# Hybrid encoder trunk on one core: other pairs of the up-projection in seven products, sums and subtractions in turn, gate convolution and silu one step later

## The chip, the cores and the metric

The kernel runs on one core of a Trainium2 chip. The metric is the device time of one execution in microseconds (us). A core has TensorE (PE in the profile; its weight loads are a row of their own, PEld), VectorE (DVE), ScalarE (ACT), GpSimd (POOL) and SyncE (SP), which issues most of the DMAs. Each engine works through a queue of its own in order and waits for the others by semaphores. On-chip memory has 128 partitions; matmuls add up in PSUM tiles (`acc`, `ps`).

## The reference

Two layers over 256 positions of width 2048. Each layer is a token mixer (attention of one kind or the other) and a gated MLP with a convolution over positions. The change lies in the MLP (`conv_ffn`), the first in layer 0 (FFN0), the second in layer 1 (FFN1).

```python
def conv_ffn(h, w_up, conv_w, conv_b, w_down):
    """Gated MLP with centred depthwise conv over positions; h: [B,S,D]."""
    u = h @ w_up
    ...
    u = lax.conv_general_dilated(u, conv_w[:, None, :].astype(u.dtype), window_strides=(1,),
                                 padding=((pad, pad),), dimension_numbers=('NWC', 'WIO', 'NWC'),
                                 feature_group_count=c) + conv_b
    gate, val = jnp.split(u, 2, axis=-1)
    return (jax.nn.silu(gate) * val) @ w_down

def reference(x, a_w_qkv, a_w_o, a_q_gain, a_k_gain, b_w_qkv, b_w_o, rel_bias,
              mix_norm, ffn_norm, w_up, conv_w, conv_b, w_down, final_norm):
    h = x
    for i in range(DEPTH):
        hn = rms_norm(h, mix_norm[i])
        j = i // N_MIXERS
        if i % N_MIXERS == 0:
            h = h + mixer_a(hn, a_w_qkv[j], a_w_o[j], a_q_gain[j], a_k_gain[j])
        else:
            h = h + mixer_b(hn, b_w_qkv[j], b_w_o[j], rel_bias)
        h = h + conv_ffn(rms_norm(h, ffn_norm[i]), w_up[i], conv_w[i], conv_b[i], w_down[i])
    return rms_norm(h, final_norm)
```

All inputs and the output are float32.

## The kernel before

**Split matmuls.** Every float32 operand is split into a rounded part and a remainder, and a product is made of three matmuls: rounded by rounded, rounded by remainder, remainder by rounded (lines 130 to 132, and 184 to 186 in a unit). Weights arrive by DMA as `raw`, tiles of 128 x 1024. For each tile ACT copies the rounded part (`wh`, lines 142 and 177) and VectorE subtracts it from `raw` to get the remainder (`wl`, lines 143 and 178; a "subtraction", S below). There are four buffers of `wh` and of `wl` and four of `raw`, with a few more in the MLP. These two instructions have a raised priority (`AHEAD`), so that the scheduler puts them ahead of work that the program states earlier; each engine's order is settled when the program is built.

**Feeds.** `feed` takes one group of 512 weight rows (a k-group, `kg`) by 512 columns: two tiles of `raw`, 24 matmuls. A plain pair of the up-projection is a block of 512 gate columns (four feeds) and the block of 512 value columns that belongs to it (four feeds), 192 matmuls. There are 11 pairs, numbered 0 to 10, worked in two halves (`HALVES`): pairs 0 to 5, then the part of the down-projection that reads them, then pairs 6 to 10 and theirs.

**Units.** For the pairs that `UP` names, `up_pair` replaces the two feeds of k-group 0, 48 matmuls, by one `fast_unit` of 42: seven products of 2 x 2 blocks in the manner of Strassen and Winograd, out of seven weights. Four of the seven are sums of raw tiles, made in place by VectorE (line 176; a "sum", A below). The order within such a pair (`UP_ORDER`) is gate k-groups 1, 2, 3, the unit, value k-groups 1, 2, 3. The seven products are put together by VectorE in PSUM and in `fold` (lines 690 to 698). On the side of the activations the unit needs recombined inputs of k-group 0 (`picks`), which `sums` prepares once per half with small VectorE rows (lines 649 and 657).

**The work behind the matmuls.** When a gate block is summed up, `gate_gen` evacuates it (ACT, line 486, into `stg`), turns it (`turned`: two transposes of VectorE, line 374, and 16 copies of POOL, line 559, into `u`), and goes on with the value of the pair before: its convolution (ACT line 538, VectorE line 546) and its product with the gate (line 574). When a value block is summed up, `value_gen` evacuates and turns it, waits a number of steps, convolves the gate of its own pair, applies silu (line 583), and splits the product of the pair before for the down-projection (`act_split`, lines 601 and 602). In the last pair of each half, half of the copies that turn the value go to ACT (line 561). For two k-groups of the down-projection in each half (`fast`: those of pairs 1 and 2, 7 and 8) `act_split` calls `combined` instead, which forms differences (line 612) and splits them (lines 317 and 318, tiles `s`, `sx` and `c`), since the down-projection works these two k-groups with `fast_unit` too.

**What sets the order.** These generators advance at each `yield`. A feed calls `step` two times for the oldest of the waiting generators, a unit three times; when one is done, the next one's turn comes. How many yields stand in a generator thus says how many half feeds later a piece is stated in the program. The scheduler then orders each engine's queue by what is stated, by priority and by data.

Of the kernel before, what the change touches and what calls it, by code (L numbers as in the profile page):

```python
# [22 lines left out]
SCALE = 128.0 ** -0.5  # L23
NRAW, NHL = 4, 4
AHEAD = 60
UP = 1, 4, 6, 7, 10
UP_ORDER = (1, 0), (2, 0), (3, 0), (0, None), (1, 1), (2, 1), (3, 1)
NWARM = 11
QC = [(q, c) for q in range(4) for c in range(4)]
# [4 lines left out]
def tile_encoder(ctx: ExitStack, tc: tile.TileContext, x, xT, w_a, w_ao, q_gain, k_gain, w_b, w_bo,  # L34
                 rel_bias, gains, w_up, conv, w_down, final_norm, rope, ident_c, onehot, out):
    nc = tc.nc
# [64 lines left out]
    def raw_tile():  # L101
# [4 lines left out]
            return pool.tile([P, 2, 512], F32, tag=tags[0], name=nm("raw"), bufs=2 if len(tags) == 1 else 1)  # L106
        return spool.tile([P, 2, 512], F32, tag="raw", name=nm("raw"), bufs=NRAW)

    def of_m(x, m):
        return x[m] if isinstance(x, tuple) else x[:, m * P:(m + 1) * P]  # L110

    def feed(accs, lhs, kg, wap, first, last, by_m=False, pieces=1, mid=None, begun=()):
        raws, w = [], 2048 // pieces
        for i in range(max(pieces, 2)):
            if pieces < 4 or i % 2 == 0:
                raws.append(raw_tile())
            w = min(w, 1024)
            r = raws[-1].rearrange("p a c -> p (a c)")
            k = i % 2 if pieces == 4 else 0
            nc.sync.dma_start(r[:, k * w:(k + 1) * w], wap[:, i * w:(i + 1) * w])  # L120
            if mid is not None:
                mid(i)

        def mms(order):
            for m, kt in order:
                (wh, wl), j = hls[kt // 2], kt % 2
                xh, xl = lhs[4 * kg + kt][:2]
                st, sp = first and kt == 0 and m not in begun, last and kt == 3
                xh, xl = of_m(xh, m), of_m(xl, m)
                nc.tensor.matmul(accs[m], xh, wh[:, j, :], start=st, stop=False)  # L130
                nc.tensor.matmul(accs[m], xh, wl[:, j, :], start=False, stop=False)  # L131
                nc.tensor.matmul(accs[m], xl, wh[:, j, :], start=False, stop=sp)  # L132

        hls = []
        for s in range(2):
            wh = spool.tile([P, 2, 512], F32R, tag="wh", name=nm("wh"), bufs=NHL)
            wl = spool.tile([P, 2, 512], F32R, tag="wl", name=nm("wl"), bufs=NHL)
            r = raws[s]
            with tc.high_priority(offset=AHEAD):
                for i in range(max(pieces // 2, 1)):  # L140
                    c = slice(i, i + 1) if pieces == 4 else slice(0, 2)
                    nc.scalar.activation(wh[:, c], r[:, c], AF.Copy)  # L142
                    nc.vector.tensor_tensor(wl[:, c], r[:, c], wh[:, c].bitcast(F32), ALU.subtract)  # L143
            hls.append((wh, wl))
            if not by_m:
                for kt in (2 * s, 2 * s + 1):
                    mms([(m, kt) for m in range(2)])
                    step(kt % 2 == 0)
        if by_m:
            mms([(m, kt) for m in range(2) for kt in range(4)])  # L150
# [11 lines left out]
    def fast_unit(acc, pick, wap0, wap1, begun, end, spot):  # L162
        def load(wap, i):
            r = raw_tile()
            nc.sync.dma_start(r.rearrange("p a c -> p (a c)"), wap[:, i * 1024:(i + 1) * 1024])
            return r

        b11, b21, b22, b12 = load(wap0, 0), load(wap0, 1), load(wap1, 1), load(wap1, 0)
        t1, t2, t4 = (b11, b22, b21) if spot is None else (spot(i) for i in range(3))
        sums = {3: (t1, b11, b12), 5: (b12, b12, b22), 7: (t2, t1, b22), 6: (t4, t2, b21)}  # L170
        for i, (q, r) in enumerate(((1, b11), (2, b21), (3, b22), (5, t1), (7, b12), (6, t2), (4, t4))):
            wh = spool.tile([P, 2, 512], F32R, tag="wh", name=nm("wh"), bufs=NHL)
            wl = spool.tile([P, 2, 512], F32R, tag="wl", name=nm("wl"), bufs=NHL)
            with tc.high_priority(offset=AHEAD):
                if q in sums:
                    nc.vector.tensor_tensor(*sums[q], ALU.add)  # L176
                nc.scalar.activation(wh, r, AF.Copy)  # L177
                nc.vector.tensor_tensor(wl, r, wh.bitcast(F32), ALU.subtract)  # L178
            xh, xl = pick[q]
            for j in range(2):  # L180
                st = q not in begun and j == 0
                sp = q in end and j == 1
                a, b = (x[j] if isinstance(x, tuple) else x[:, j] for x in (xh, xl))
                nc.tensor.matmul(acc[q], a, wh[:, j], start=st, stop=False)  # L184
                nc.tensor.matmul(acc[q], a, wl[:, j], start=False, stop=False)  # L185
                nc.tensor.matmul(acc[q], b, wh[:, j], start=False, stop=sp)  # L186
            begun.add(q)
            step(i % 2 == 0)
# [300 lines left out]
    def ffn(l, hT, ss_in, cw, g_next, last, side=None):  # L489
        with tc.tile_pool(name=nm("fpool"), bufs=1) as fp:  # L490
# [44 lines left out]
            def conv(blk):  # L535
                n, u, c = blk
                for j in range(4):
                    tc.keep_in_program_order(nc.scalar.activation(  # L538
                        halves(c[:, j]), u[:, j, :, :P], AF.Identity, bias=tap(n, j, 3), scale=tap(n, j, 1)))
                    if j == 1:  # L540
                        yield
                flat = u.rearrange("p j m t -> p j (m t)")
                for j in range(4):
                    cj = halves(c[:, j])
                    for i, o in ((0, 0), (2, 1)):
                        nc.vector.scalar_tensor_tensor(cj, halves(flat[:, j, o:o + NT])[:, ::-1], tap(n, j, i), cj,  # L546
                                                       ALU.mult, ALU.add)
                    if j == 1:
                        yield
# [13 lines left out]
            def gate_gen(accs, blk, value):  # L563
                s = evac_scaled(fp, accs, rstd, 1)
                yield
                turned(s, blk[1])
                if value is not None:
                    yield
                    yield from product(value)

            def product(value):
# [4 lines left out]
            def value_gen(accs, blk, gate, last):  # L576
                s = evac_scaled(fp, accs, rstd, 1)
                yield
                turned(s, blk[1], blk[0] - NPAIR in (HALVES[0][1] - 1, NPAIR - 1))
                for _ in range(3 if gate[0] in UP else 1 if last else 4):  # L580
                    yield
                yield from conv(gate)
                nc.scalar.activation(gate[2], gate[2], AF.Silu)
                if last is not None:
                    yield
                    yield from act_split(last)
# [59 lines left out]
            def sums(kg, at, r, st):  # L646
                hts = [hT[4 * kg + j][:2] for j in range(4)]
                for j, (hi, lo) in enumerate(hts):
                    nc.vector.tensor_tensor(r[:, j], hi.bitcast(F32), lo.bitcast(F32), ALU.add)
                    if j == 1:  # L650
                        yield
                v = r.rearrange("p (b j) (m t) -> p b j m t", b=2, m=2)
# [854 lines left out]
```

## Time and profile before

| what | value |
|---|---|
| median of 3 runs | 2250.79 us (2250.02 to 2251.2) |
| profiled execution | 2250.06 us, span 2248.3 us, mean granted clock 0.998 |
| VectorE: subtractions of feeds, x708 | 887.1 us busy, mean 1264 ns |
| VectorE: subtractions of units out of raw tiles, x126 | 154.8 us busy, mean 1256 ns |
| POOL: copies that turn gate and value, x672 | 519.4 us busy, mean 773 ns |
| DMA from HBM | 432.34 MB read, 195 GB/s over the span |

Times are microseconds unless marked ns. A row of the timeline gives start, duration, engine, line and operation, output and inputs, shapes, how many rows of one kind it merges (x4), and in brackets the idle time before it with what ended it. A row of the waits gives the waiting engine and line, what it waited for, the idle time in total, how often, and the longest. A row of the windows gives the stretch, its length, the busy time of PE, PEld, DVE, ACT and POOL with counts, the granted clock of TensorE, the share of the DMA engines and GB/s. A row of the groups gives busy time, mean ns of one, and idle time before them. Matmul starts are what tells TensorE's pace, since matmuls overlap.

### The profile page before, as it was taken

Reading aid. Unit: us, or ns where it says so; the run is one execution under the profiler, and the core shown is the slowest. Engines: PE = TensorE matmul, PEld = TensorE weight load, DVE = VectorE, ACT = ScalarE, POOL = GpSimd, SP = SyncE. Lnnn points to the kernel's source line nnn. Section 1 sums busy time; section 2 is a strip of 40 time slices with the busy share of each in tenths; the row PEclk is TensorE's granted clock in tenths of the full one; section 3 lists DMA queues with packets and bytes.
Section 4 is the critical chain, followed back from the end, with each engine's and each line's share of the span. In section 5 each row is a group of like instructions: output and inputs, shape, how many; then the busy total and the mean of one; then the engine's idle time right before and its main releaser. Section 6 shows DMA issues by size and latency. Waiting matters only on the chain.

```text
span 2248.3 us, 28923 instructions
## 1 busy us (share of the span) xinstructions
PE 2217.8 (99%) x9945; PEld 1833.1 (82%) x9945; DVE 1905.6 (85%) x2415; ACT 1351.5 (60%) x1902; POOL 761.5 (34%) x1017
## 2 busy tenths in 40 slices
PE   9999999999999999999999999999999999999998
PEld 7888878888887887888888888888788878878877
DVE  6877779898899989868886878687999998898987
ACT  7676665666455656665454455566666755565664
POOL 2343236652005662040053006003665500347511
PEclk9999999999999999999999999999999999999999
DMA  8565655556556546565556555556455555556654
GB/s 303 193 217 175 218 184 201 184 199 195 205 190 208 192 163 212 198 187 197 189 186 196 179 187 184 195 185 212 171 205 196 193 198 197 200 189 202 208 187 142
DMA packets 126181, 439.60 MB, mean 196 GB/s; under 512 B 14408, under 2 KB 18248, under 8 KB 126032
## 3 DMA queue, kind: packets, MB, share of 16 engines
q1 hardware_dynamic: 123056, 429.05, 56.5%
q0 software_dynamic: 2688, 8.39, 1.5%
q8 instruction: 78, 1.28, 0.2%
q14 instruction: 71, 0.58, 0.1%
q10 hardware_dynamic: 288, 0.30, 0.0%
HBM read 432.34 MB, written 5.34 MB: 195 GB/s over the span
## 4 chain that ended last, share of the span: by engine, by line
PE 46%; DVE 5%; issue 2%; DMA 1%; POOL 1%; ACT 1%; DVEq 0%; POOLq 0%; ACTq 0%
PE acc L132 13%; PE acc L130 13%; PE acc L131 13%; DVE wl L143 2%; PE ps L185 1%; PE ps L186 1%; PE ps L184 1%; DVE wl L178 1%; DMA raw<-in_w_b_dram 1%; PE acc L185 1%; PE acc L186 1%; DMA raw<-in_w_up_dram 1%; PE acc L184 1%; DVE raw L176 1%; ACT wh L142 1%
## 5 line engine op out<-in xcount | busy, mean ns | idle before, releaser
L143 DVE TENSOR_TENSOR wl<-raw,wh 128x1024 fp32r<-128x1024 f32 (+1 forms) x708 | 887.1, 1264 | 192.6 <-ACT wh L142 187.7
L142 ACT ACTIVATE wh<-raw 128x1024 fp32r<-128x1024 f32 (+1 forms) x708 | 738.9, 1048 | 505.7 <-PE acc L132 393.9
L131 PE MATMUL acc<-wl,xh 128*128 128x512 f32 x2016 | 785.6, 390 | 1.7 <-DVE wl L143 1.7
L130 PE MATMUL acc<-wh,xh 128*128 128x512 f32 x2016 | 786.3, 390 | 0.7 <-ACT wh L142 0.7
L132 PE MATMUL acc<-wh,xh 128*128 128x512 f32 x2016 | 784.5, 389 | 0.0
L559 POOL COPY u<-quad 32x256 f32<-32x256 f32 x672 | 519.4, 773 | 451.8 <-DVE quad L374 414.9
L131 PEld LDWEIGHTS acc<-wl,xh 128*128 128x128 f32 x2016 | 378.6, 188 | 80.6 <-DVE wl L143 4.1
L130 PEld LDWEIGHTS acc<-wh,xh 128*128 128x128 f32 x2016 | 378.8, 188 | 78.5 <-ACT wh L142 1.1
L132 PEld LDWEIGHTS acc<-wh,xh 128*128 128x128 f32 x2016 | 378.5, 188 | 78.8
L130 PE MATMUL acc<-wh,a 128*128 128x512 f32 x720 | 281.7, 391 | 1.6 <-ACT a L601 1.6
L132 PE MATMUL acc<-wh,a 128*128 128x512 f32 x720 | 281.0, 390 | 0.6 <-DVE a L602 0.6
L131 PE MATMUL acc<-wl,a 128*128 128x512 f32 x720 | 281.0, 390 | 0.0
L177 ACT ACTIVATE wh<-raw 128x1024 fp32r<-128x1024 f32 x126 | 133.2, 1060 | 115.0 <-PE acc L132 95.8
L130 PEld LDWEIGHTS acc<-wh,a 128*128 128x128 f32 x720 | 135.8, 189 | 30.0 <-ACT a L601 2.5
L132 PEld LDWEIGHTS acc<-wh,a 128*128 128x128 f32 x720 | 135.5, 188 | 29.7 <-DVE a L602 1.4
L131 PEld LDWEIGHTS acc<-wl,a 128*128 128x128 f32 x720 | 135.6, 188 | 28.2 <-DVE wl L143 0.4
L178 DVE TENSOR_TENSOR wl<-raw,wh 128x1024 fp32r<-128x1024 f32 x126 | 154.8, 1256 | 1.5 <-ACT wh L177 0.9
L378 POOL COPY wide<-quad 32x256 f32<-32x256 f32 x133 | 90.1, 678 | 168.2 <-DVE quad L374 159.8
L395 POOL COPY wide<-quad 32x256 f32<-32x256 f32 x88 | 53.1, 603 | 240.2 <-DVE quad L374 173.0
L546 DVE SCALAR_TENSOR_TENSOR cg<-u,cw,cg 128x256 f32<-128x256 f32 x176 | 88.3, 542 | 11.3 <-ACT cg L538 11.0
L486 ACT ACTIVATE stg<-acc,rstd 128x512 f32<-128x512 f32 x122 | 80.5, 680 | 24.7 <-DVE acc L693 12.1
L546 DVE SCALAR_TENSOR_TENSOR cv<-u,cw,cv 128x256 f32<-128x256 f32 x176 | 85.4, 532 | 0.0
(309 smaller groups left out, 2275.5 us busy)
## 6 DMA issues: line engine op xcount, KB each, us to landing
raw<-in_w_up_dram SPq DMA_DIRECT2D x352, 512.0 KB, 4.6
raw<-in_w_down_dram SPq DMA_DIRECT2D x176, 512.0 KB, 4.5
raw<-in_w_b_dram SPq DMA_DIRECT2D x144, 512.0 KB, 4.4
raw<-in_w_bo_dram SPq DMA_DIRECT2D x48, 512.0 KB, 4.4
raw<-in_w_a_dram SPq DMA_DIRECT2D x40, 512.0 KB, 4.7
raw<-in_w_ao_dram SPq DMA_DIRECT2D x32, 512.0 KB, 4.6
raw<-in_w_a_dram SPq DMA_DIRECT2D x16, 256.0 KB, 5.8
there<-quad POOLq DMA_DIRECT2D x6, 512.0 KB, 4.0
```

Source lines behind the costliest of these rows:

```text
L130: nc.tensor.matmul(accs[m], xh, wh[:, j, :], start=st, stop=False)
L131: nc.tensor.matmul(accs[m], xh, wl[:, j, :], start=False, stop=False)
L132: nc.tensor.matmul(accs[m], xl, wh[:, j, :], start=False, stop=sp)
L142: nc.scalar.activation(wh[:, c], r[:, c], AF.Copy)
L143: nc.vector.tensor_tensor(wl[:, c], r[:, c], wh[:, c].bitcast(F32), ALU.subtract)
L177: nc.scalar.activation(wh, r, AF.Copy)
L178: nc.vector.tensor_tensor(wl, r, wh.bitcast(F32), ALU.subtract)
L378: nc.gpsimd.tensor_copy(o[32 * c:32 * c + 32, :, 32 * q:32 * q + 32], quad[32 * q:32 * q + 32, c])
L395: nc.gpsimd.tensor_copy(dst, src)
L486: nc.scalar.activation(o[:, m, :], accs[m], AF.Copy, scale=rstd[:, m:m + 1])
L546: nc.vector.scalar_tensor_tensor(cj, halves(flat[:, j, o:o + NT])[:, ::-1], tap(n, j, i), cj, ALU.mult, ALU.add)
L559: nc.gpsimd.tensor_copy(o, src)
```

## The change

`UP` names pairs 2, 4, 6, 7 and 8 instead of 1, 4, 6, 7 and 10: five units per layer as before, three of them in a row in the second half. In the units of the up-projection each sum is issued after the subtraction before it (`issue_after`), and `sums` ties its four additions behind the newest subtraction of a feed. In `gate_gen` the value of pair 0 is convolved one step later. In `value_gen` the number of steps ahead of the gate's convolution becomes 4 instead of 3 for a unit's pair, 2 instead of 1 for a plain pair with another before it in its half, and 5 instead of 4 for a plain pair that opens a half; one step more stands ahead of silu.

```diff
-UP = 1, 4, 6, 7, 10
+UP = 2, 4, 6, 7, 8
...
+    newest = [None]
...
-                    nc.vector.tensor_tensor(wl[:, c], r[:, c], wh[:, c].bitcast(F32), ALU.subtract)
+                    newest[0] = nc.vector.tensor_tensor(wl[:, c], r[:, c], wh[:, c].bitcast(F32), ALU.subtract)
...
                 if q in sums:
-                    nc.vector.tensor_tensor(*sums[q], ALU.add)
+                    with tc.issue_after(done.ins) if spot is None else ExitStack():
+                        nc.vector.tensor_tensor(*sums[q], ALU.add)
                 nc.scalar.activation(wh, r, AF.Copy)
-                nc.vector.tensor_tensor(wl, r, wh.bitcast(F32), ALU.subtract)
+                done = nc.vector.tensor_tensor(wl, r, wh.bitcast(F32), ALU.subtract)
...
                 if value is not None:
-                    yield
+                    for _ in range(2 if blk[0] == 1 else 1):
+                        yield
                     yield from product(value)
...
-                for _ in range(3 if gate[0] in UP else 1 if last else 4):
+                for _ in range(4 if gate[0] in UP else 2 if last else 5):
                     yield
                 yield from conv(gate)
+                yield
                 nc.scalar.activation(gate[2], gate[2], AF.Silu)
...
                 for j, (hi, lo) in enumerate(hts):
-                    nc.vector.tensor_tensor(r[:, j], hi.bitcast(F32), lo.bitcast(F32), ALU.add)
+                    with tc.issue_after(newest[0].ins):
+                        nc.vector.tensor_tensor(r[:, j], hi.bitcast(F32), lo.bitcast(F32), ALU.add)
```

The counts of instructions are the same on every engine, and so is the order of SP's DMA issues. In the changed file line numbers are two to six higher: L145 and L181 are the subtractions, L179 the sum, L541 and L549 the convolution, L698 to L704 the fold, L607 the split.

VectorE in the unit of pair 7 in FFN0, before (`cg` rows are the convolution of the gate of pair 6, L374 the transposes, L692 the first row of the unit's fold):

```order
L546 SCALAR_TENSOR_TENSOR cg_5960<-u_5955,cw_555,cg_5960 128x256 x2
L178 TENSOR_TENSOR wl_6481<-raw_6472,wh_6480 128x1024
L176 TENSOR_TENSOR raw_6472<-raw_6472,raw_6478 128x1024
L176 TENSOR_TENSOR raw_6478<-raw_6478,raw_6476 128x1024
L178 TENSOR_TENSOR wl_6491<-raw_6474,wh_6490 128x1024
L178 TENSOR_TENSOR wl_6501<-raw_6476,wh_6500 128x1024
L176 TENSOR_TENSOR raw_6476<-raw_6472,raw_6476 128x1024
L176 TENSOR_TENSOR raw_6474<-raw_6476,raw_6474 128x1024
L178 TENSOR_TENSOR wl_6512<-raw_6472,wh_6511 128x1024
L178 TENSOR_TENSOR wl_6523<-raw_6478,wh_6522 128x1024
L178 TENSOR_TENSOR wl_6534<-raw_6476,wh_6533 128x1024
L178 TENSOR_TENSOR wl_6545<-raw_6474,wh_6544 128x1024
```

and now:

```order
L549 SCALAR_TENSOR_TENSOR cg_5960<-u_5955,cw_555,cg_5960 128x256 x4
L181 TENSOR_TENSOR wl_6476<-raw_6467,wh_6475 128x1024
L181 TENSOR_TENSOR wl_6486<-raw_6469,wh_6485 128x1024
L179 TENSOR_TENSOR raw_6467<-raw_6467,raw_6473 128x1024
L181 TENSOR_TENSOR wl_6500<-raw_6471,wh_6499 128x1024
L179 TENSOR_TENSOR raw_6473<-raw_6473,raw_6471 128x1024
L181 TENSOR_TENSOR wl_6511<-raw_6467,wh_6510 128x1024
L179 TENSOR_TENSOR raw_6471<-raw_6467,raw_6471 128x1024
L181 TENSOR_TENSOR wl_6523<-raw_6473,wh_6522 128x1024
L179 TENSOR_TENSOR raw_6469<-raw_6471,raw_6469 128x1024
L181 TENSOR_TENSOR wl_6534<-raw_6471,wh_6533 128x1024
L698 TENSOR_TENSOR acc_6324<-acc_6324,junk_6554 128x512
```

The sums stand singly between subtractions; the fourth subtraction moved from the eighth place to the sixth, the sixth kept the tenth, and the first row of the fold, which stood behind the seventh, stands ahead of it.

VectorE in pair 8 of FFN0, before, where the pair is plain (`cg` is the gate of pair 7, `a` the split of pair 6's product):

```order
L143 TENSOR_TENSOR wl_6835<-raw_6810,wh_6834 128x1024
L546 SCALAR_TENSOR_TENSOR cg_6322<-u_5954,cw_555,cg_6322 128x256 x4
L143 TENSOR_TENSOR wl_6860<-raw_6855,wh_6859 128x1024
L602 TENSOR_TENSOR a_6875<-cv_5961,a_6875 128x256 x2
L143 TENSOR_TENSOR wl_6882<-raw_6857,wh_6881 128x1024
L602 TENSOR_TENSOR a_6876<-cv_5961,a_6876 128x256 x2
L143 TENSOR_TENSOR wl_6911<-raw_6906,wh_6910 128x1024
```

and now, as a unit:

```order
L145 TENSOR_TENSOR wl_6831<-raw_6810,wh_6830 128x1024
L549 SCALAR_TENSOR_TENSOR cg_6322<-u_5954,cw_555,cg_6322 128x256 x4
L181 TENSOR_TENSOR wl_6865<-raw_6856,wh_6864 128x1024
L549 SCALAR_TENSOR_TENSOR cg_6322<-u_5954,cw_555,cg_6322 128x256 x3
L181 TENSOR_TENSOR wl_6875<-raw_6858,wh_6874 128x1024
L179 TENSOR_TENSOR raw_6856<-raw_6856,raw_6862 128x1024
L181 TENSOR_TENSOR wl_6889<-raw_6860,wh_6888 128x1024
L179 TENSOR_TENSOR raw_6862<-raw_6862,raw_6860 128x1024
L181 TENSOR_TENSOR wl_6900<-raw_6856,wh_6899 128x1024
L179 TENSOR_TENSOR raw_6860<-raw_6856,raw_6860 128x1024
L181 TENSOR_TENSOR wl_6912<-raw_6862,wh_6911 128x1024
L179 TENSOR_TENSOR raw_6858<-raw_6860,raw_6858 128x1024
```

Three rows of the convolution stand between the unit's first two subtractions, and four sums come where the pair had none.

ACT at the end of the up-projection of FFN0's second half, before, where pair 10 is a unit (`cg` is its gate, `stg` the evacuation of its value):

```order
L142 ACTIVATE wh_7913<-raw_7876 128x1024
L142 ACTIVATE wh_7941<-raw_7937 128x1024
L538 ACTIVATE cg_7466<-u_5954,cw_555 128x256 x2
L142 ACTIVATE wh_7962<-raw_7939 128x1024
L486 ACTIVATE stg_7869<-acc_7470,rstd_2629 128x512
L486 ACTIVATE stg_7869<-acc_7471,rstd_2629 128x512
```

and now:

```order
L144 ACTIVATE wh_7913<-raw_7876 128x1024
L541 ACTIVATE cg_7491<-u_5954,cw_555 128x256 x4
L144 ACTIVATE wh_7945<-raw_7941 128x1024
L489 ACTIVATE stg_7869<-acc_7691,rstd_2629 128x512
L489 ACTIVATE stg_7869<-acc_7692,rstd_2629 128x512
```

All four rows of the gate's convolution stand ahead of the value's evacuation, one weight copy earlier than the first two stood.

## Prediction

> **What bounds the kernel now.** I read the page's busy times and its chain first.
>
> ```profile
> span 2248.3 us, 28923 instructions
> PE 2217.8 (99%) x9945; PEld 1833.1 (82%) x9945; DVE 1905.6 (85%) x2415; ACT 1351.5 (60%) x1902; POOL 761.5 (34%) x1017
> PE 46%; DVE 5%; issue 2%; DMA 1%; POOL 1%; ACT 1%; DVEq 0%; POOLq 0%; ACTq 0%
> ```
>
> TensorE sets the end. Another engine costs time only where a matmul finds its operand unready, so I listed the waits of PE around each unit and at the two ends of an up-projection. FFN0, pairs 1, 7 and 10 and the end:
>
> ```profile
> PE ps L185 <- DVE wl L178: 2.1, 1, 2.1
> PE acc L185 <- DVE wl L178: 0.6, 1, 0.6
> ...
> PE ps L185 <- DVE wl L178: 1.7, 1, 1.7
> ...
> PE ps L185 <- DVE wl L178: 0.3, 1, 0.3
> ...
> PE acc L130 <- ACT a L601: 1.6, 1, 1.6
> PE acc L131 <- DVE wl L143: 1.2, 1, 1.2
> PE acc L132 <- DVE a L602: 0.3, 1, 0.3
> PE acc L130 <- ACT wh L142: 0.2, 1, 0.2
> ```
>
> FFN1 repeats the rows of pairs 7 and 10. Its pair 1 has the 0.6 and the first row below; its end has the 1.2, the 0.3 and the second row:
>
> ```profile
> PE ps L185 <- DVE wl L178: 2.0, 1, 2.0
> ...
> PE acc L130 <- ACT wh L142: 0.7, 1, 0.7
> ```
>
> Idle: 2.7 + 1.7 + 0.3 + 3.3 = 8.0 us in FFN0, 2.6 + 1.7 + 0.3 + 2.2 = 6.8 in FFN1, in 8 and 7 waits. A wait costs more than its idle time, as the matmuls around pair 7's show:
>
> ```profile
> 709.47 0.39 PE L184 MATMUL ps<-wh,s 128*128 128x512 f32 x1
> 711.52 0.50 PE L185 MATMUL ps<-wl,s 128*128 128x512 f32 x1 [1.66 <-DVE wl L178]
> 711.86 0.39 PE L186 MATMUL ps<-wh,s 128*128 128x512 f32 x1
> ```
>
> Undisturbed starts are 0.227 us apart (705.39 to 705.62 below). Here they are 2.05 and 0.34: 1.94 lost for 1.66 idle, so 0.27 more per wait. 14.8 idle + 15 × 0.27 = 18.9 us.
>
> The end of the up-projection holds one more loss: the granted clock.
>
> ```profile
> 863.00:907.00 44.00, 40.61 (x168) 32.27 (x168) 36.01 (x52) 31.84 (x56) 12.59 (x22) 0.96 0.51 171
> 2130.00:2174.00 44.00, 41.81 (x174) 33.23 (x173) 37.88 (x52) 28.67 (x47) 10.90 (x15) 0.96 0.50 167
> ...
> 2146.73 0.63 PE L132 MATMUL acc<-wh,sx 128*128 128x512 f32 x1
> 2147.16 0.63 PE L130 MATMUL acc<-wh,sx 128*128 128x512 f32 x1
> ```
>
> The next to last column is 0.96; matmuls there start 0.43 apart, 0.2 above nominal. 0.04 × 44 is 1.8; I take 1.6 per layer. What this change can touch thus holds 18.9 + 3.2 = **22.1 us**; the rest of the 2248.3 is matmuls at their pace and stages that the diff leaves alone.
>
> **Removed.** Pair 1 is plain now: 2.7 + 2 × 0.27 = 3.2 us per layer go. Pair 10 is plain: 0.6 goes. The end costs 4 × 0.27 + 3.3 + 1.6 = 6.0 and 3 × 0.27 + 2.2 + 1.6 = 4.6. Its cause:
>
> ```profile
> 867.32 1.09 ACT L538 ACTIVATE cg<-u,cw 128x256 f32<-128x256 f32 x2 [5.68 <-DVE acc L698]
> 854.17 13.12 POOL L559 COPY u<-quad 32x256 f32<-32x256 f32 x16 [15.09 <-DVE quad L374]
> ```
>
> The releaser named is not the real one: the convolution starts as POOL's last copy of pair 10's gate ends, 854.17 + 13.12 = 867.29. ACT stands 5.68 us, and behind it in its queue stand the next weight copies, the last evacuation and the splits that the down-projection reads. A unit delivers its gate after the fold, with three value feeds to go: 72 × 0.227 = 16.3 us. A plain pair delivers it four feeds ahead, 21.8 us, and without the fold. POOL then ends 5 to 8 us sooner, about as much as ACT stood. The convolution's extra step does not bite here: pair 10 waited three steps as a unit; now two before the convolution and one before silu. I take 0 for the end; at worst all 10.6 us stay.
>
> **Added: the split's order.** The engines issue as many instructions as before, DMAs included, and SP's queue keeps its order; only waits can differ. VectorE in the third unit of FFN0 (pair 7):
>
> ```profile
> 705.39 0.39 PE L184 MATMUL ps<-wh,xh 128*128 128x512 f32 x1
> 705.62 0.39 PE L185 MATMUL ps<-wl,xh 128*128 128x512 f32 x1
> ...
> 693.93 1.05 DVE L546 SCALAR_TENSOR_TENSOR cg<-u,cw,cg 128x256 f32<-128x256 f32 x2 [1.09 <-ACT cg L538]
> 695.37 1.40 DVE L143 TENSOR_TENSOR wl<-raw,wh 128x1024 fp32r<-128x1024 f32 x1 [0.39 <-ACT wh L142]
> 701.24 1.42 DVE L178 TENSOR_TENSOR wl<-raw,wh 128x1024 fp32r<-128x1024 f32 x1
> 702.69 2.64 DVE L176 TENSOR_TENSOR raw<-raw,raw 128x1024 f32<-128x1024 f32 x2
> 705.26 2.55 DVE L178 TENSOR_TENSOR wl<-raw,wh 128x1024 fp32r<-128x1024 f32 x2
> 707.84 2.48 DVE L176 TENSOR_TENSOR raw<-raw,raw 128x1024 f32<-128x1024 f32 x2
> 710.25 4.62 DVE L178 TENSOR_TENSOR wl<-raw,wh 128x1024 fp32r<-128x1024 f32 x4
> 714.78 0.69 DVE L692 TENSOR_TENSOR acc<-acc,junk 128x512 f32<-128x512 f32 x1
> ```
>
> Seven subtractions S and four sums A, each 1.16 to 1.42 us; the unit's seven weights are used every 6 × 0.227 = 1.36 us. One A between two S makes 2.3 (4.62 / 2) to 2.64 us per weight, so VectorE falls 1 us behind with each, whatever the order; its lead pays. Before, the order was S A A S S A A S S S S and the fourth S came eighth; after, S S A S A S A S A S, fold, S: the fourth S comes sixth, the sixth still tenth, the seventh behind a fold row of 0.6.
>
> **Pair 7.** The fourth S, 2.5 us earlier, no longer stalls; the seventh decides. It ended at 714.87 and is needed at 705.39 + 6 × 1.36 + 0.23 = 713.8. The fold adds 0.6; the idle 1.09 and 0.39, which the convolution one step later would not meet, take 1.48 away: 714.0 to 715.5, I take 714.5, a loss of 0.7 + 0.33 = 1.0 (range 0.3 to 1.9) instead of 1.9.
>
> **Pair 8** is a unit now, the third in a row. In before VectorE runs from 714.87 to this subtraction with 0.34 us of idle time:
>
> ```profile
> 747.18 1.41 DVE L143 TENSOR_TENSOR wl<-raw,wh 128x1024 fp32r<-128x1024 f32 x1
> 748.52 1.15 DVE L602 TENSOR_TENSOR a<-cv,a 128x256 fp32r<-128x256 f32 x2
> ...
> 749.74 0.39 PE L131 MATMUL acc<-wl,xh 128*128 128x512 f32 x1
> ```
>
> 33.7 us, and it is used at 749.74, 1.1 after its end. The unit starts where this feed did, at 749.51 less the 0.9 that pair 7 saves: 748.6. Up to the unit's second S there is one more subtraction (1.33), one fold row less (0.6) and perhaps no idle time (0.34): 714.5 + 33.7 + 1.33 − 0.6 − 0.34 = 748.6. Four pairs of A and S (9.2 to 10.6), half of the 1.15 us row of splits and the last S (1.16 to 1.42) end at 759.6 to 761.2; needed at 748.6 + 8.2 + 0.2 = 757.0. With 0.33 for the refill the loss is 2.9 to 4.5; I take **3.7**, the largest term.
>
> **Pair 4** has no wait in a row of its own. Ahead of its unit stood these:
>
> ```profile
> 440.39 1.23 DVE L318 TENSOR_TENSOR s<-st,s 128x1024 fp32r<-128x1024 f32 x1 [0.74 <-ACT s L317]
> 442.87 1.41 DVE L318 TENSOR_TENSOR sx<-cv,sx 128x512 fp32r<-128x512 f32 x2
> ```
>
> One step later they fall among its sums: up to 1.23 + 1.41 = 2.6 more where no lead is left, less what VectorE does earlier in their place. Bounds 0.3 to 2.9; I take 1.5.
>
> **Pair 2** follows a plain pair like pair 4, with splits of L602 (1.15 for two) inside, less what the earlier fourth S gains: 1.0 (0.5 to 1.6). **Pair 6** had no stall: 0.3 (0 to 0.9).
>
> **Pairs 3 and 9** are plain, but come behind a unit that eats the lead, and in them the fast k-groups of the down-projection are split:
>
> ```profile
> L612 DVE TENSOR_TENSOR st<-cv,st 128x256 f32<-128x256 f32 x16 | 9.8, 613 | 0.0
> L318 DVE TENSOR_TENSOR s<-st,s 128x1024 fp32r<-128x1024 f32 x8 | 10.0, 1249 | 5.2 <-ACT s L317 5.2
> L318 DVE TENSOR_TENSOR sx<-cv,sx 128x512 fp32r<-128x512 f32 x8 | 7.0, 879 | 0.0
> ```
>
> 4 × 0.61 + 1.25 + 0.88 + one more 0.61 = 5.2 in place of four splits, 2 × 1.15 = 2.3. The 2.9 more stand against the 1.1 us by which pair 8 cleared its feed behind pair 7: up to 1.8 lost at once, or nothing where the lead has come back. 1.0 each (0 to 2.5).
>
> The four sums of 0.5 us that the first k-group's preparation now ties behind a subtraction cost nothing: they run several feeds ahead of pair 6's unit or before the first pair; without that cover, 4 × 0.5 us once per layer.
>
> **Sum.** Added per layer: 1.0 + 1.0 + 1.5 + 0.3 + 1.0 + 3.7 + 1.0 = 9.5; both 19.0. Removed 22.1. Net −3 us: the profiled execution took 2250.06 (span 2248.3 and 1.8 around it), so 2247.0; the median of the runs shown, 2250.79, is 0.7 above it, so **2247.8**. All low ends: 0.5 + 0 + 0.3 + 0 + 0.3 + 2.9 + 0 = 4.0, −14. All high ends: 1.6 + 2.5 + 2.9 + 0.9 + 1.9 + 4.5 + 2.5 = 16.8, +11.5 with the end still gone.
>
> On the clock there is a rule. The Trainium skill, "TensorE: Matmul & The Clock Gate", section "Why this matters for your kernels", asks for "No PE-idle gaps >~3µs between matmul bursts"; by it no wait here, before or after, would lower the clock. The 0.43 us spacing right behind idle times of 0.66 and 1.24 us in FFN1 does not bear that out. By the rule the sum stays 2247.8; by the trace, pair 8's three or four waits of about 1 us could set it off as well, 1.6 per layer, 2251.0.
>
> **Rivals.** *VectorE has more lead than I give it.* For it: the idle rows ahead of pairs 4, 7 and 8 (0.74, 1.09 and 0.39, 0.34) are waits for ACT, which a later convolution avoids. Against: the 4.62 us row shows it saturated inside. Every unit gains a microsecond or more: pair 8 down to 2.4, pair 4 to 0.8, pair 7 to 0.3, pair 2 to 0.5, pairs 3, 6 and 9 to 0: 4.0 × 2 − 22.1 = −14, some 2237.
>
> *Three units in a row saturate VectorE (slower).* Place: pairs 7 to 9. A unit's eleven rows take 12.8 to 15.6 us (at 1.16 and 1.42) where TensorE's seven weights take 9.5; if POOL's copies run through the units, every row is at the upper end, nothing comes back before pair 9's combined split, pairs 8 and 9 take 4.5 and 2.5, pair 4 its 2.9, the clock drops at pair 8 (1.6), pair 7 keeps 1.9: 1.0 + 1.0 + 2.9 + 0.3 + 1.9 + 6.1 + 2.5 = 15.7 per layer, +9: 2260. With the other terms as forecast it decides from a loss of 5.3 us at pair 8: there the time is that of before.
>
> *The end stays.* Later convolutions leave the last splits late, and half to all of 10.6 us remains: 2253 to 2258. Against: pair 10's step count is unchanged and POOL is through sooner.
>
> *The order is not what the diff says:* the listing of the changed program shows S and A in turn; no chance.
>
> **How the numbers follow.** Forecast, 2243 to 2253: 0.57. More lead, 2234 to 2242: 0.19. Saturation, 2253 to 2262: 0.13. The end stays: 0.11. About 0.2%, 4.5 us, is what a measurement of this kernel can tell from no change. Below 2246.3: 0.23 of the forecast's and the 0.19, **0.42**. Above 2255.3: 0.09 + 0.06, **0.15**. Between: **0.43**. The range leaves out a tenth on each side: **2240 to 2255**.
>
> **What would show it.** Right: no wait at pair 1, at pair 10 or at the first matmuls of the down-projection; granted clock 1.00 in those windows; waits on L185's counterpart of 3 to 4 us at pair 8, all on the last subtractions, and about 1 us at pairs 2, 4 and 7. Wrong: a wait on ACT's splits at the end; ACT idle behind POOL there; pair 8 under 2 us (then the time is near 2237) or waits all through pair 9 (then 2260).

## The result, and the profile after

The changed kernel takes 2248.30 us in the median of 20 runs (2245.41 to 2251.9); the kernel before, run beside it, 2253.38 in 20 (2249.36 to 2257.74). The ratio is **0.9979, 95% interval 0.9972 to 0.9986**: 3 to 6 us less. The two profiled executions stand only 1.9 us apart (spans 2248.3 and 2246.4), since the one of before is among its kernel's shortest; the traces below therefore show where the time lies, and the ratios show how much it is.

The page of the changed kernel, its span, busy times and chain:

```profile
span 2246.4 us, 28935 instructions
PE 2220.4 (99%) x9945; PEld 1830.8 (81%) x9945; DVE 1902.1 (85%) x2415; ACT 1350.8 (60%) x1902; POOL 745.0 (33%) x1017
PE 43%; DVE 9%; issue 2%; DMA 1%; ACT 1%; POOL 1%; DVEq 0%; POOLq 0%; ACTq 0%
```

Counts are as before. VectorE has a larger share of the chain, 9% against 5%: in the up-projections the waits that are left are on it, or on one of ACT's copies for a unit, which wait for its sums. The waits of PE by window in FFN0, pairs 2, 3, 4 (two rows), 6, 7 and 8:

```profile
PE ps L188 <- DVE wl L181: 0.2, 1, 0.2
...
PE acc L133 <- DVE wl L145: 0.5, 2, 0.3
...
PE acc L187 <- ACT wh L180: 0.6, 1, 0.6
PE ps L188 <- DVE wl L181: 0.2, 1, 0.2
...
PE ps L188 <- DVE wl L181: 0.2, 1, 0.2
...
PE ps L188 <- DVE wl L181: 1.2, 2, 0.6
...
PE ps L188 <- DVE wl L181: 2.7, 3, 1.0
```

Pair 8 is now the costliest place. The windows at the two ends of the up-projection, the same stretches as before, hold no wait and a full clock (third column from the end, 1.00 against 0.96):

```profile
863.00:907.00 44.00, 44.00 (x196) 36.44 (x195) 34.73 (x51) 34.96 (x60) 8.28 (x16) 1.00 0.62 191
2130.00:2174.00 44.00, 44.00 (x196) 36.44 (x195) 37.69 (x48) 29.72 (x46) 8.83 (x10) 1.00 0.59 191
```

The cause that was named for the stall there, ACT standing behind POOL's copies of pair 10's gate, is gone. The timelines of POOL and ACT at the same place:

```profile
847.67 12.70 POOL L562 COPY u<-quad 32x256 f32<-32x256 f32 x16 [7.15 <-DVE quad L377]
...
863.21 2.07 ACT L541 ACTIVATE cg<-u,cw 128x256 f32<-128x256 f32 x4
```

POOL ends at 860.4, 6.9 us sooner than before, and the convolution starts at 863.2 with no idle time ahead of it.

Below, "loss" is the excess of matmul starts over their 0.227 us, added up at one place, as in the prediction (idle time, refill and slow clock together). Each cell holds FFN0 / FFN1:

| place | before | foretold for the change | changed kernel |
|---|---|---|---|
| pair 1 | 3.2 / 3.2 | 0 | 0 / 0 |
| pair 2 | 0 / 0 | 1.0 | 0.4 / 0.5 |
| pair 3 | 0 / 0 | 1.0 | 1.0 / 0.9 |
| pair 4 | 0.3 / 0.3 | 1.5 | 1.4 / 1.5 |
| pair 6 | 0 / 0 | 0.3 | 0.5 / 0.5 |
| pair 7 | 1.9 / 2.3 | 1.0 | 2.1 / 2.5 |
| pair 8 | 0 / 0 | 3.7 | 3.8 / 3.8 |
| pair 9 | 0 / 0 | 1.0 | 0.4 / 0.4 |
| pair 10 | 0.6 / 0.6 | 0 | 0 / 0 |
| end | 6.0 / 4.9 | 0 | 0 / 0 |

In the changed kernel the places sum to 9.6 / 10.1, 19.7 in all, where 19.0 were foretold; before, they sum to 12.0 / 11.3, 23.3 in all, where 22.1 were counted. By place, these two traces thus account for 3.6 of the 3 to 6 us.

One execution fixes a place only to about 1 us. Four of the kernels below differ from the changed one only from the middle of pair 7 on, and up to there the queues of VectorE, ACT and POOL are the same, instruction for instruction; yet pair 3 of FFN0 loses 0.7 to 1.6 us in them. In the two of them that leave pair 7 as it is, it loses 2.1 and 2.9 in FFN0 and 3.4 and 2.0 in FFN1, where the changed kernel has 2.1 and 2.5.

### The profile page after: what moved, and what is told of

It reads as the page before. It is cut to its first block, busy times and chain, and to the rows that moved or that the text cites. A ratio compares the mean times of both kernels' runs of the same rounds, so it can differ in the third digit from the quotient of the medians.

```text
span 2246.4 us, 28935 instructions
## 1 busy us (share of the span) xinstructions
PE 2220.4 (99%) x9945; PEld 1830.8 (81%) x9945; DVE 1902.1 (85%) x2415; ACT 1350.8 (60%) x1902; POOL 745.0 (33%) x1017
## 4 chain that ended last, share of the span: by engine, by line
PE 43%; DVE 9%; issue 2%; DMA 1%; ACT 1%; POOL 1%; DVEq 0%; POOLq 0%; ACTq 0%
PE acc L133 13%; PE acc L132 13%; PE acc L134 13%; DVE wl L145 3%; DVE wl L181 2%; DVE raw L179 1%; DMA raw<-in_w_b_dram 1%; PE ps L188 1%; PE ps L189 1%; PE ps L187 1%; DVE cv L549 1%; DMA raw<-in_w_down_dram 0%; DVE tT L386 0%; PE acc L188 0%; PE acc L187 0%
## 5 line engine op out<-in xcount | busy, mean ns | idle before, releaser
L145 DVE TENSOR_TENSOR wl<-raw,wh 128x1024 fp32r<-128x1024 f32 (+1 forms) x708 | 882.6, 1258 | 199.6 <-ACT wh L144 194.5
L562 POOL COPY u<-quad 32x256 f32<-32x256 f32 x672 | 503.1, 749 | 463.3 <-DVE quad L377 426.2
L181 DVE TENSOR_TENSOR wl<-raw,wh 128x1024 fp32r<-128x1024 f32 x126 | 156.9, 1248 | 8.5 <-ACT wh L180 7.9
L549 DVE SCALAR_TENSOR_TENSOR cg<-u,cw,cg 128x256 f32<-128x256 f32 x176 | 92.7, 570 | 3.3 <-ACT cg L541 3.2
L549 DVE SCALAR_TENSOR_TENSOR cv<-u,cw,cv 128x256 f32<-128x256 f32 x176 | 90.0, 565 | 0.2
```

The source lines that it names most:

```text
L145: newest[0] = nc.vector.tensor_tensor(wl[:, c], r[:, c], wh[:, c].bitcast(F32), ALU.subtract)
L181: done = nc.vector.tensor_tensor(wl, r, wh.bitcast(F32), ALU.subtract)
L562: nc.gpsimd.tensor_copy(o, src)
```

## The experiments

Ratios are to the kernel before, from runs beside it.

### Each part alone, and in twos

The change has three parts: the pairs, the turns of sums and subtractions, the later convolution and silu. The first four kernels take the pairs alone, the turns alone, the later work alone, and the last two together. The edit of the first is a line; the others are the diff's remaining lines.

```diff
-UP = 1, 4, 6, 7, 10
+UP = 2, 4, 6, 7, 8
```

> The kernel before with the pairs of the change (2, 4, 6, 7, 8) and nothing else. My theory (the end stall hangs on pair 10 being a unit): no wait over 0.5 us at the end of either up-projection, pair 1 and pair 10 clean; units cost as much or more than in the changed kernel, since a fourth subtraction still stands eighth: pair 7 about 1.9, pair 8 3.5 to 5 us per layer. Ratio to before 0.997 to 1.000. Rival A (the later convolution cured the end): 4.6 to 6 us per layer stay there, ratio 1.001 to 1.004.

> The kernel before with sums and subtractions in turn and nothing else. My theory: only units change; pair 1's wait of 2 us on the fourth subtraction shrinks to about 1 us, pair 7's 1.9 to 0.7 to 1.9; the end stays at 4.6 to 6 us per layer. Ratio 0.998 to 1.000. Rival B (the order of the sums is the main gain): ratio 0.9965 or less.

> The kernel before with the convolution and silu one step later and nothing else. My theory: the end stays or grows (pair 10, a unit, now waits 4 steps and one more ahead of silu): 5 to 8 us per layer; units lose or gain less than 1 us. Ratio 0.999 to 1.003. Rival A: the end falls under 1 us per layer, ratio 0.995 to 0.997.

> The changed kernel with the pairs of before (1, 4, 6, 7, 10). My theory: the end stays at 5 to 8 us per layer, pair 1 and pair 7 lose 1 to 2 us each; ratio 0.998 to 1.002. Rival A: end under 1 us per layer, ratio 0.994 to 0.997.

| kernel | ratio, 95% interval | loss at the end, FFN0 / FFN1 |
|---|---|---|
| pairs alone | 1.0042, 1.0029 to 1.0055 | 0 / 0 |
| turns alone | 1.0000, 0.9992 to 1.0009 | 6.0 / 3.6 |
| later alone | 1.0014, 1.0005 to 1.0022 | 5.3 / 6.6 |
| turns and later, old pairs | 1.0009, 0.9999 to 1.0019 | 5.1 / 5.7 |

The end stall follows pair 10: wherever pair 10 is a unit it stays, and with the pairs alone it is gone. Rival A, that the later convolution cured it, falls. That pair 10's unit is the condition is shown; that the way from there to the stall is ACT standing behind POOL is read from the traces and was not varied alone. ACT's wait at this place in FFN0 is 5.7 us before, 3.7 with the turns, 4.0 with the later work and 4.7 with both, and the loss does not follow it, so another part of the unit's late work may share in it. But the pairs alone make the kernel *slower*, by 0.42%, which neither theory had: my range ended at 1.000. The turns alone changed pair 1 hardly (3.0 where "about 1 us" was written) and raised pair 7 to 3.0 / 3.2; they are worth nothing by themselves.

Where do the pairs alone lose? Losses are 4.6 us at pair 3, 4.9 at pair 4, 4.9 at pair 7 and 5.5 at pair 8 in FFN0, and 1.0, 4.5, 1.9 and 4.8 in FFN1. Pairs 4, 7 and 8 of FFN0 and pair 4 of FFN1 each hold 1.6 us of slow clock (last section). Pair 3 is a plain pair. POOL, ACT and VectorE of that kernel ahead of it in FFN0:

```profile
380.58 15.39 POOL L559 COPY u<-quad 32x256 f32<-32x256 f32 x16 [17.41 <-DVE quad L374]
...
396.00 1.09 ACT L538 ACTIVATE cg<-u,cw 128x256 f32<-128x256 f32 x2 [6.14 <-POOL u L559]
397.00 1.24 ACT L486 ACTIVATE stg<-acc,rstd 128x512 f32<-128x512 f32 x2
398.14 1.05 ACT L142 ACTIVATE wh<-raw 128x1024 fp32r<-128x1024 f32 x1
...
397.70 1.30 DVE L374 STREAM_TRANSPOSE quad<-stg 128x512 f32<-128x512 f32 x2 [2.92 <-ACT stg L486]
```

This is the picture of the end stall again, at another unit. The gate of pair 2 comes late (after the unit's fold), POOL copies it until 395.97, the convolution stands at the head of ACT's queue for 6.14 us, and behind it the evacuation of pair 2's value and the next weight copy, which starts at 398.14. VectorE stands 2.92 us for that evacuation, with nothing to subtract, and then has everything at once. In FFN1 ACT stood 3.74 us at this place, and pair 3 lost 1.0. So the next two kernels asked which of the other parts the new pairs need.

> The changed kernel without the turns of sums and subtractions (its pairs and its later convolution). Theory D (the new pairs need the later convolution, since the split of pairs 1 and 7 and the convolutions fall into the plain pair behind a unit): the 4.6 us at pair 3 seen with the pairs alone fall under 1.5 us; units still lose 2 to 5 us each on the fourth subtraction; ratio to before 0.999 to 1.002. Rival E (the new pairs need the turns): pairs 3 and 9 keep over 3 and 2 us, ratio 1.003 or more.

> The changed kernel without the later convolution (its pairs and its turns). Theory D: pair 3 keeps 3.5 to 5 us and pair 9 2 us per layer, units 4, 7 and 8 lose 1 to 2 us less than with the pairs alone; ratio 1.000 to 1.003. Rival E: pair 3 under 1.5 us, ratio under 0.999.

Pairs and later work: 0.9984, 0.9975 to 0.9992. Pairs and turns: **1.0055**, 1.0043 to 1.0068. Theory D holds, more strongly than its numbers: the pairs need the later work (in FFN0 pair 3 loses 1.6 with it against 4.1 us without, pair 8 3.3 against 6.3, pair 9 0.8 against 2.7), and without it the turns do not help. Of the 6.3 us, 2.6 are matmuls at the slow clock. Its forecast that the fourth subtraction would still cost every unit 2 to 5 us was wrong for pairs 2, 4, 6 and 7 (0.5, 1.1, 0 and 1.8 in FFN0) and right for pair 8 alone (3.3 / 4.9). The same place in the kernel with pairs and later work:

```profile
394.66 0.69 ACT L486 ACTIVATE stg<-acc,rstd 128x512 f32<-128x512 f32 x1 [4.77 <-DVE acc L699]
395.25 1.05 ACT L142 ACTIVATE wh<-raw 128x1024 fp32r<-128x1024 f32 x1
...
397.99 1.10 ACT L538 ACTIVATE cg<-u,cw 128x256 f32<-128x256 f32 x2 [1.12 <-POOL u L559]
```

Evacuation and weight copy now stand ahead of the convolution, and 1.12 us of its wait are left. ACT still stands 4.77 us before them, for VectorE's fold; what is gained is the weight copy, which starts at 395.25 instead of 398.14. Over the whole span, the waits of ACT's gate convolution (line, what it waited for: us in total, times, longest) are, before:

```profile
ACT cg L538 <- DVE acc L698: 30.1, 8, 6.1
ACT cg L538 <- POOL u L559: 17.0, 10, 3.1
```

with the pairs alone:

```profile
ACT cg L538 <- POOL u L559: 29.3, 9, 6.1
ACT cg L538 <- DVE acc L698: 22.1, 7, 5.3
```

and in the changed kernel:

```profile
ACT cg L541 <- POOL u L562: 7.9, 7, 2.5
ACT cg L541 <- DVE acc L704: 4.3, 2, 2.1
```

These are 47.1, 51.4 and 12.2 us; in the kernel with pairs and turns, the slowest of all, they are 61.2. The sum alone does not order the kernels: the turns alone have 58.4 and take as long as the kernel before. Most waits of up to 3.7 us hide under VectorE's lead (with the turns alone, twelve of 2.6 to 3.7 us stand in plain pairs with no loss of TensorE behind them); the one of 6.14 us at pair 3 and the one of 5.68 at the end do not.

### What pair 8 and pair 7 cost

The unit saves 6 matmuls, 1.36 us, and pair 8 loses 3.8. Two kernels have four units per layer.

```diff
-UP = 2, 4, 6, 7, 8
+UP = 2, 4, 6, 7
```

> The changed kernel with four units per layer (2, 4, 6, 7): pair 8 is plain, 6 more matmuls of 0.227 us per layer. My theory (the third unit in a row finds no lead): its 3.75 us per layer go, 1.36 come, pair 9 no worse: 4.8 us less than the changed kernel, ratio to before 0.995 to 0.997. Rival C (VectorE lacks time over pairs 7 to 9 as a whole, and what it does not owe in pair 8 it owes in pair 9): the waits move to pairs 8 and 9, ratio 0.998 to 1.000.

```diff
-UP = 2, 4, 6, 7, 8
+UP = 2, 4, 6, 8
```

> The changed kernel with four units per layer (2, 4, 6, 8): pair 7 plain, pair 8 a unit behind a plain pair. My theory: pair 7's 2.1 to 2.5 us go, pair 8's 3.75 fall to 0.5 to 1.5 as in pairs 2 and 4, 1.36 come: 6 to 9 us less than the changed kernel over both layers, ratio to before 0.994 to 0.996. Rival C: pair 8 or 9 still loses 3 us, ratio 0.997 to 0.999.

Pair 8 plain: **0.9955**, 0.9941 to 0.9968. Pair 7 plain: **0.9949**, 0.9936 to 0.9961, 2242.18 us in the median of 5 runs. With fewer units, both beat the changed kernel and the one before, and rival C falls: with pair 8 plain no wait of TensorE is left in pairs 8 to 10 of FFN0. The waits of PE with pair 7 plain, pair 8's window and pair 9's:

```profile
PE ps L188 <- DVE wl L181: 0.2, 1, 0.2
...
PE acc L133 <- DVE wl L145: 0.7, 3, 0.3
```

Pair 8 as a unit behind a plain pair loses 0.5 us in either layer instead of 3.8; pair 9 loses 1.6 / 1.7, 1.2 more than in the changed kernel, so a part of the load did move there; it stays within the range foretold for a plain pair with a combined split behind a unit (1.0, up to 2.5).

Why does the third unit in a row cost that much? Rival "saturation" in the prediction named POOL's copies. The next kernel leaves out those that turn pair 7's value.

```diff
                 for i, (q, c) in enumerate(QC):
...
+                    if blk == NPAIR + 7:
+                        continue
```

> The changed kernel with the 16 POOL copies that turn pair 7's value left out (one turn per layer; stale values are convolved). These run from the last gate feed of pair 8 to the middle of its unit, and VectorE's rows there take 1.41 instead of 1.21 us. Theory H (the slower rows are a part of pair 8's loss): rows of 1.2 us from the end of pair 8's gate feeds on, about ten rows by 0.2 us, pair 8 loses 1.5 to 2.2 instead of 3.75. Rival I (the number of rows alone decides, VectorE would only wait for ACT or TensorE instead): pair 8 keeps 3.2 us or more.

VectorE in pair 8's unit, the changed kernel:

```profile
751.97 1.41 DVE L181 TENSOR_TENSOR wl<-raw,wh 128x1024 fp32r<-128x1024 f32 x1
753.31 1.41 DVE L179 TENSOR_TENSOR raw<-raw,raw 128x1024 f32<-128x1024 f32 x1
754.64 1.42 DVE L181 TENSOR_TENSOR wl<-raw,wh 128x1024 fp32r<-128x1024 f32 x1
...
759.79 1.21 DVE L181 TENSOR_TENSOR wl<-raw,wh 128x1024 fp32r<-128x1024 f32 x1
```

and without the copies:

```profile
752.07 1.22 DVE L181 TENSOR_TENSOR wl<-raw,wh 128x1024 fp32r<-128x1024 f32 x1
753.21 1.22 DVE L179 TENSOR_TENSOR raw<-raw,raw 128x1024 f32<-128x1024 f32 x1
754.34 1.22 DVE L181 TENSOR_TENSOR wl<-raw,wh 128x1024 fp32r<-128x1024 f32 x1
```

In the changed kernel the rows take 1.41 us until POOL is through (742.72 to 757.66) and 1.21 after; without the copies 1.22 throughout, and pair 8 loses 1.2 us in both layers, under the 1.5 to 2.2 of theory H, far under rival I's 3.2. VectorE does the same 21 rows in both, from the end of the two transposes to the end of the last subtraction: they take 19.9 us in the changed kernel and 17.2 without the copies, in either layer. So two thirds of pair 8's loss, 2.6 us, are VectorE's rows slowed beside POOL. That the remaining 1.2 are the number of rows fits, but their number was not varied.

Pair 7 lost 2.1 / 2.5 us where 1.0 was foretold. VectorE of the changed kernel there:

```profile
696.38 2.12 DVE L549 SCALAR_TENSOR_TENSOR cg<-u,cw,cg 128x256 f32<-128x256 f32 x4 [1.39 <-ACT cg L541]
...
704.05 1.23 DVE L181 TENSOR_TENSOR wl<-raw,wh 128x1024 fp32r<-128x1024 f32 x1 [0.74 <-ACT wh L180]
...
715.49 1.21 DVE L181 TENSOR_TENSOR wl<-raw,wh 128x1024 fp32r<-128x1024 f32 x1
```

Two idle times are in it. The second is ACT's weight copy, which stands behind silu of pair 6's gate, and silu behind VectorE's convolution:

```profile
702.01 1.06 ACT L588 ACTIVATE cg<-cg 128x1024 f32<-128x1024 f32 x1 [2.28 <-DVE cg L549]
702.98 1.99 ACT L180 ACTIVATE wh<-raw 128x1024 fp32r<-128x1024 f32 x2
```

The next kernel leaves this silu out.

```diff
-                nc.scalar.activation(gate[2], gate[2], AF.Silu)
+                if gate[0] != 6:
+                    nc.scalar.activation(gate[2], gate[2], AF.Silu)
```

> The changed kernel with silu of pair 6's gate left out (one ACT row of 1.06 us per layer, which stands in ACT's queue between the first and the second weight copy of pair 7's unit and waits there for VectorE's convolution; the values behind it are wrong). Theory F (this row is why pair 7 loses 2.1 to 2.5 us and not 1.0): VectorE's idle 0.74 us ahead of the second subtraction goes, every later subtraction of pair 7 ends 0.6 to 0.8 us sooner, pair 7 loses 1.2 to 1.8; pair 8 still 3.4 to 4.0. Rival G (pair 7 is short of VectorE time whatever ACT does): pair 7 within 0.2 us of the changed kernel.

The idle 0.74 is gone, but the seventh subtraction ends only 0.5 us sooner (716.2 for 716.7), since more of the rows now fall beside POOL's copies at 1.42; pair 7 loses 1.8 in FFN0 and 3.0 in FFN1. Theory F falls as the whole explanation.

The first idle time, in which the convolution waits for ACT and ACT for POOL, differs between executions, and the loss follows it. The row after it with pair 8 plain (FFN1) and without the copies for pair 7 (FFN0), where the queues up to here are those of the changed kernel:

```profile
1958.63 2.12 DVE L549 SCALAR_TENSOR_TENSOR cg<-u,cw,cg 128x256 f32<-128x256 f32 x4 [2.76 <-ACT cg L541]
...
698.05 2.12 DVE L549 SCALAR_TENSOR_TENSOR cg<-u,cw,cg 128x256 f32<-128x256 f32 x4 [2.26 <-ACT cg L541]
```

Over both layers of these three kernels this idle time and the loss of pair 7 are 1.38 and 2.0 us, 1.39 and 2.1 (twice), 1.85 and 2.5, 2.26 and 2.9, 2.76 and 3.4: the loss grows with the idle time one for one. Without silu they are 1.40 and 1.8, 2.76 and 3.0, so silu's row is worth 0.3 to 0.4 us, and the first idle time is the larger part. Nothing was tried that removes it.

### The turns, and the step ahead of silu

> Four units (2, 4, 6, 8) with the later convolution, without the turns of sums and subtractions. If the turns are worth 0.5 us per unit or more, 3 to 5 us above the same with turns, ratio to before 0.996 to 0.9975; if they are worth nothing here, since the last subtractions stand where they stood, ratio 0.994 to 0.996.

The edit is the list of pairs 2, 4, 6, 8 in the kernel with pairs and later work. The ratio is 0.9965, 0.9951 to 0.9978, against 0.9949, 0.9936 to 0.9961 with turns; the intervals overlap, and the two profiled spans are 2240.3 and 2240.4. Whether the turns are worth anything stays open. In the traces the turns cost 0.5 us at pair 6 and 0.3 to 0.5 at pair 4, and the down-projection behind the first half loses 1.6 / 0.9 with them against 2.5 / 2.5 without.

```diff
                 yield from conv(gate)
-                yield
                 nc.scalar.activation(gate[2], gate[2], AF.Silu)
```

> The changed kernel without the extra step ahead of silu. The scheduler puts silu behind the convolution on VectorE that it needs, and in pair 7 at the same place in ACT's queue with or without the step. My theory: no effect of its own, ratio to before 0.997 to 0.999, pairs 7 and 8 as in the changed kernel. Rival: the splits that follow silu come a step sooner and meet the units: pair 4 or 8 over 1 us worse, ratio 0.9995 or more.

0.9997, 0.9989 to 1.0006: without this one step nearly the whole gain is gone, and my theory of no effect falls. The rival's mechanism is not shown either: pairs 4 and 8 lose 1.6 and 4.0 in FFN0, 0.2 and 0.3 more than with the step. The profiled execution is 4.0 us longer, spread over many waits: pairs 2, 3, 7 and 9 of FFN0 lose 0.2, 0.7, 0.5 and 0.6 more, the down-projections behind the first halves 0.3 and 0.7. Differences of this size at one place also occur between executions of one order, so they locate nothing by themselves. One thing can be read at pair 3, where four rows of the combined split stand in one piece ahead of a subtraction; with the step there are two rows on each side of one:

```profile
409.07 1.15 DVE L616 TENSOR_TENSOR st<-cv 128x256 f32<-128x256 f32 x2
410.14 1.08 DVE L616 TENSOR_TENSOR st<-cv,st 128x256 f32<-128x256 f32 x2
411.14 1.22 DVE L145 TENSOR_TENSOR wl<-raw,wh 128x1024 fp32r<-128x1024 f32 x1
```

That subtraction came 0.35 us late for its matmul; with the step no matmul waited there. One cause for the whole was not found.

## Why the prediction was right, and where it was not

The forecast was 2247.8 us with a range of 2240 to 2255; 2248.3 was measured. That the two lie 0.5 us apart is in part luck. The forecast took 3.0 us off 2250.79, the median of three runs; in the runs beside the changed kernel the median of before is 2253.38, and the gain 5.1 us. Two pairs of errors also cancel in the sum: pair 7 lost 1.1 and 1.5 us more than its term, pairs 2 and 9 together 1.2 and 1.1 less.

- **The end of the up-projection** (10.6 us, the largest gain): right in size (10.9), and four kernels show that it goes with pair 10's unit, as written. The way from there, through ACT and POOL, rests on the traces.
- **Pairs 1 and 10**: no wait is left, as written.
- **Pair 8** (3.7, the largest loss): 3.8 in both layers, and right in its working too. Pair 7's last subtraction ended at 716.7, not 714.5, but TensorE came later as well: pair 8's unit started at 750.3, not 748.6. Counted from that start, the last subtraction ended after 12.2 us, where the forecast has 11.0 to 12.6. What it left open is how much of this is POOL: two thirds of the loss.
- **Pair 4** (1.5) and **pair 3** (1.0) came out as foretold, pair 4 with two rows of the combined split among its sums and subtractions, as written; **pairs 2 and 9** (1.0 each) came out at 0.4 to 0.5.
- **Pair 7** is the step that failed: "the idle 1.09 and 0.39, which the convolution one step later would not meet, take 1.48 away". VectorE met 1.39 and 0.74 instead in FFN0, and 1.85 and 0.74 in FFN1: the convolution, a step later, still waited for POOL's copies. The first idle time counts in full, the second for 0.3 to 0.4. The loss of 2.1 to 2.5 lies outside the range of 0.3 to 1.9, and so do the other four that the same order gave (2.0 to 3.4).
- **The later convolution's role** was misread, though the sum does not show it. It was priced as a move that loads some units and spares others idle time. It is what the new pairs stand on: with them the later work takes the ratio from 1.0055 to 0.9979 (turns in both), of which the step ahead of silu is 0.9997 to 0.9979; without them it costs 0.14%. The prediction had the mechanism, ACT at a standstill behind a unit's late gate, but saw it at pair 10 alone; it looked at what the trace of before shows and did not ask where else a unit's gate would meet an early convolution.
- **The rivals**: saturation by POOL's copies was real (1.41 us rows, two thirds of pair 8's loss) but pair 8 stayed at 3.8, under the 5.3 from which it would have decided. The clock did not drop at pair 8; with waits of 1.0, 1.0 and 0.6 us inside 8 us the window's granted clock is 1.00, and the alternative of 2251.0 falls. The Trainium skill ("TensorE: Matmul & The Clock Gate", section "Why this matters for your kernels") asks for no idle gaps over about 3 us between bursts of matmuls; by that no drop comes here either. The other traces of this case do not bear it out: with pairs and later work the clock dropped at pair 8 of FFN1 behind waits of 0.7 and 2.1 us. The last section shows what the drops follow, and that pair 8 of FFN0 missed one narrowly: this part was luck.
- On the sign the text gave 0.42 to faster and 0.43 to no change; the measured 0.21%, 0.14 to 0.28, lies on the line between the two.

## What to carry to other kernels

In an in-order queue a late producer stalls everything behind the waiting instruction, as ACT's 6.14 us at pair 3 show. Before a stage that delivers late (here a unit whose gate comes after a fold) is moved, find the instruction that waits for its output at each new place and count what stands behind it; here one step later in the program was worth 0.76% with the new pairs, and the turns of sums and subtractions inside the unit nothing that could be told from no change. And a saving per use has a capacity: a unit that saves 1.4 us of TensorE pays where VectorE has lead, and the fifth one, third in a row, cost 3.8.

## What the runs showed of the hardware

VectorE's 128 x 1024 rows take 1.41 us beside POOL's copies and 1.21 without, in the same unit of the same kernel; leaving out 16 copies per layer shortened pair 8 by 2.6 us.

The granted clock of TensorE dropped on shorter idle times than the 3 us that the prediction quotes. With the pairs alone, pair 4 idles 0.55 and then 2.31 us, and right after it matmuls start 0.43 apart:

```profile
455.78 0.50 PE L185 MATMUL acc<-wl,xh 128*128 128x512 f32 x1 [0.55 <-DVE wl L178]
...
461.13 0.50 PE L185 MATMUL ps<-wl,s 128*128 128x512 f32 x1 [2.31 <-DVE wl L178]
...
462.54 0.63 PE L184 MATMUL ps<-wh,s 128*128 128x512 f32 x1
462.96 0.63 PE L185 MATMUL ps<-wl,s 128*128 128x512 f32 x1
```

No single gap there reaches 3 us, nor does their sum. What the drops follow can be worked out from the traces of all kernels. A drop halves the clock for 3.41 us (6.83 once, where the first 3.41 held 0.9 us more of idle time), and within one trace the drops start whole multiples of 3.413 us apart: with the pairs alone at 462.3, 721.7, 769.5 and 1732.0, which is 76, 14 and 282 stretches. So each trace can be cut into such stretches, and the idle time of TensorE in each be added up from the brackets of its rows. The 20 stretches that a drop follows hold 1.76 to 2.50 us. Of 61 others with more than 1.0 us, 60 hold at most 1.76 us, and one holds 1.93. So what counts in these traces is idle time of about half a stretch, on a grid that the waits do not shift. The end of the up-projection of FFN0 before, with 1.92 us in the first stretch and the granted clock in the third column from the end:

```profile
886.90:890.30 3.40, 1.48 (x6) 0.85 (x6) 3.40 (x7) 2.13 (x5) 0.00 (x0) 1.00 0.47 160
890.30:893.70 3.40, 3.40 (x10) 2.63 (x9) 2.59 (x3) 1.10 (x2) 0.00 (x0) 0.50 0.69 220
893.70:897.10 3.40, 3.40 (x17) 2.79 (x16) 2.13 (x3) 1.57 (x2) 0.00 (x0) 1.00 0.66 231
```

A single gap of 2.06 us in pair 1 of the same trace, ending at 324.56, brought no drop: a boundary at 323.7 splits it. Pair 8 of FFN0 in the changed kernel held 1.75 us in one stretch, at the edge; pair 8 of FFN1, with the same waits on another part of the grid, held 1.02. Whether a given wait costs 1.6 us more is thus also a matter of where it falls on the grid, and the grid lies differently in each trace.
